# A branch prefetch hint, a new order of the up/gate steps, and the general path moved, in the experts of a 512-token layer pair

## The chip, the core and the metric

The kernel is one program on one core of a Trainium2 chip. The time is that of the device for one execution, in microseconds (us); lower is better. Engine names: PE is TensorE (PEld its weight loads), DVE is VectorE, ACT ScalarE, POOL GpSimd, SP SyncE, which here mainly starts DMAs. A "q" behind a name (PEq) is that engine's sequencer, which takes instructions in order, runs branches, and hands the rest to the engine.

## The reference, cut to what matters

All of it is fp32: a first layer (state-space mixer, gated convolution, MLP), a second one with a delta-rule mixer, and at its end a mixture of experts. Only the last is touched by the change:

```
N_GROUPS, EXPERTS_PER_GROUP, TOP_K = 4, 8, 2          # 32 experts, T = 512 tokens, D = 1024, D_EXPERT = 512
pg_top, g_top = lax.top_k(softmax(xf @ w_group + b_group), 1)
pe_top, e_top = lax.top_k(softmax(el_g), TOP_K)        # two experts of the token's group
wts = pg_top * pe_top / sum(pe_top)
hid = silu(xb @ w_gate[e]) * (xb @ w_up[e])            # xb: the tokens that chose expert e
out[token] += (hid @ w_down[e]) * wts
```

How many tokens an expert gets depends on the data, so the kernel must handle any count.

## The kernel before

**Stages.** The dense layers take the first 1,436 us of the profiled span. Then one Python loop (line 1964 on) lays out 32 experts, one after the other, i = 0 to 31; pair p = i // 2, place in the pair h = i % 2. Here "even" experts are the first of a pair (h = 0), "odd" ones the second.

**One expert.** SP loads six chunks of 1 MB (`load`: up and gate for k 0 to 3, up and gate for k 4 to 7, two of down) into a ring of 15 chunk buffers; a chunk's DMA waits until PE has used the buffer's last content. `gate_up` (L1722) multiplies the first 64 slots of the expert by up and gate (tile `gu`, 16 fp32 matmuls, two side by side in the array), ACT takes SiLU of the gate half (L1733), DVE multiplies (L1734) into `gh`. Then comes the branch `longer` (L1891): `tc.If(nx > 0)` at L1893, where `nx` is the number of 32-slot blocks that the expert has beyond its first 64 slots. If it has none, every engine jumps over the body; if it has one, an inner branch (L1894) takes `block_up`/`block_down`; if more, `wide_up`/`wide_down`. Behind the branch `hidden` transposes `gh` on PE (tile `tr`, L1741) and ACT copies it (`hT`), `outputs` multiplies by down (tile `dn`, L1753, 8 fp32 matmuls), DVE scales the result (L1757) and POOL scatters it to DRAM (`yd`).

**What else stands behind the branch on PE.** Even experts: `per_slot` (tile `cb`, L1666) turns the one-hot matrix `oh1`, which DVE builds (`places`, L1789 and L1792), into the token list of the next pair. Odd experts: `columns` (tile `xt`, L1716) transposes the next pair's 128 gathered rows, which ACT reads (L1719), `prepare` (L1807) transposes 64 more, and two `per_slot`.

**Order.** PE's instructions keep the order in which the program is written (`manual_schedule`); on the other engines a scheduler orders them inside a block between branches. Every engine has its own copy of each branch and jumps by itself.

**The last expert.** `longest` (L1946) handles counts beyond what `longer` holds, in a branch of its own (L1948) ahead of the last expert's `gate_up`. Its body holds a loop for each of the 32 experts. `read_back` (L1942) adds the scattered outputs, read back in four chunks (`yd`), to the residual; the last pair is not scattered but added by matmuls (`combined`).

Of the kernel before, what the change touches and what calls it, by code (L numbers as in the profile page):

```python
# [84 lines left out]
class Kern:  # L85
# [1377 lines left out]
    def route(self, lt_ps, r2):  # L1463
# [12 lines left out]
        self.extra = lp.tile([1, 33], I32, name="extra")  # L1476
# [132 lines left out]
    def moe(self, out):  # L1609
# [15 lines left out]
        def t_(tag, shape, dt=F32, bufs=1, pool=mp):  # L1625
            return pool.tile(shape, dt, tag=tag, bufs=bufs, name=self.nm(tag))
# [95 lines left out]
        def gate_up(ws, xs, s0, gh, tag="gu", bufs=1, between=(), start=4):  # L1722
# [12 lines left out]
            for fn in between:  # L1735
                fn()

        def hidden(gh, put=V.tensor_copy):
            pt = p_("tr", 1)
# [57 lines left out]
        def ranks(p):  # L1797
            return self.rank[:, :, expert(2 * p):expert(2 * p) + 9:8]

        gh, gh2 = r1[:, 2], t_("gh2", [P, 512])  # L1800
        xb1 = t_("xb1", [P, 8, 64])

        def prepare(r):

            ps = p_("xt", 2)
            for k in range(8):
                M.transpose(ps[:, 64 * k:64 * k + 64], xt1[r:r + 64, k * P:k * P + P], self.ident[r:r + 64, r:r + 64])  # L1807
            return ps

        def normed(ps, xb):  # L1810
            S_ = [P, 8, 64]
            V.tensor_tensor(xb, ps.rearrange("p (k s) -> p k s", k=8), self.gs[:, 0].unsqueeze(2).broadcast_to(S_), op=ALU.mult)
            V.tensor_tensor(xb, xb, self.gs[:, 1].unsqueeze(2).broadcast_to(S_), op=ALU.add)
            return xb
# [60 lines left out]
        def vals(p):  # L1875
            return self.vals[:, :, p]

        def wide_up(ws):
            gate_up(ws, normed(prepare(64), t_("xb2", [P, 8, 64])), 0, gh2, "cb", 3)

        def wide_down(ws, w):
            for fn in combined([down(ws, hidden(gh2), w[:, 1:2], w[:, 0:1], yx, "b")]):
# [6 lines left out]
        def longer(i, ws, nx, first, xb, far):  # L1889
            w, sx = first[0], first[2]  # L1890
            if sx is not None:  # L1891
                sx = sx[:, i % 2:i % 2 + 1]
            with tc.If(nx > 0):  # L1893
                with tc.If(nx > 1) as more_:  # L1894
                    hb = block_up(ws, xb, i % 2)
                    wide_up(ws)
                    block_down(ws, w[:, i % 2], hb, i % 2, sx)
                    wide_down(ws, far[1][:, i % 2])
                    with ExitStack() as ies:
                        for b in range(1, INLINE):  # L1900
                            ies.enter_context(tc.If(nx > 1 + 2 * b))
                            far = further(per_slot(places(ranks(i // 2), 96 + 64 * b, 64, "b"), vals(i // 2)))
                            rows2(far, i % 2)
                            wide_up(ws)
                            wide_down(ws, far[1][:, i % 2])
# [24 lines left out]
        oh1, oh2 = places(ranks(0), 64, 32, "b"), places(ranks(0), 96, 64, "2")  # L1930
        firsts, far = [], None

        def ahead():
# [2 lines left out]
            firsts.append(more(0, per_slot(oh1, vals(0))))  # L1936
            far = further(per_slot(oh2, vals(0)))

        def read_back(tl, t):

            for j in range(2):
                V.tensor_add(acc[:, t], acc[:, t], tl[:, j])  # L1942

        def longest():

            last = 1 + 2 * INLINE  # L1946
            c = self.chunk
            with tc.If(most > last):  # L1948
                for i in range(32):
                    nx = length(i)  # L1950
                    with tc.If(nx > last):
                        self.chunk = c
                        ws = load(i)
                        rc = t_("rc", [P, 4, 2])
                        V.tensor_scalar(rc, ranks(i // 2), -32.0 * last, None, op0=ALU.add)
                        with tc.For_i(last, nx, 2):
                            V.tensor_scalar(rc, rc, -64.0, None, op0=ALU.add)
                            far = further(per_slot(places(rc, 0, 64, "b"), vals(i // 2)), "3")
                            rows2(far, i % 2)
                            wide_up(ws)  # L1960
                            wide_down(ws, far[1][:, i % 2])

        pair, back = [], []
        nx = length(0, engines=engs)
        for i in range(32):
            p, h = divmod(i, 2)
            if h == 0 and p < 14:
                oh = onehot(p + 2)
            ws = load(i)
            if i == 31:  # L1970
                for t in range(4):
                    if t == 3:
                        longest()
                    back.append(chunk("yd").rearrange("p (c d) -> p c d", c=2))
                    nc.sync.dma_start(back[t], self.yd.rearrange("(c t p) d -> t p c d", c=2, p=P)[t])
                for t in range(2):
                    read_back(back[t], t)
            if i:
                with tc.If(length(i, engines=[mybir.EngineType.Pool]) > 1):
                    rows2(far, h)  # L1980
            if h and p < 15:
                oh2 = places(ranks(p + 1), 96, 64, "2")
            gate_up(ws, xs, 64 * h, gh, between=[] if i else [ahead], start=4 if i else 1)
            if i == 0:
                with tc.If(length(0, engines=[mybir.EngineType.Pool]) > 1):
                    rows2(far, 0)
                xb = normed(prepare(0), xb1)
            nx0, nx = nx, length(i + 1, engines=engs) if i < 31 else None
            longer(i, ws, nx0, firsts[p], xb, far)
            if h == 0 and p < 15:  # L1990
                oh1 = places(ranks(p + 1), 64, 32, "b")
            pw = pw1 = pw2 = ps = None
            if h and p < 15:
                columns()
                ps = prepare(0)
                if p < 14:
                    pw = per_slot(oh, vals(p + 2))
            hT = hidden(gh, A.copy)
            if p < 15:
                if h == 0:  # L2000
                    pw1 = per_slot(oh1, vals(p + 1))
                else:
                    pw2 = per_slot(oh2, vals(p + 1))
            w, sx = wv[p]
            if p < 15:
                scatter(sx[:, h:h + 1], outputs(ws, hT, w[:, h, 1:2]), 2)
            else:
                pair.append(down(ws, hT, w[:, h, 1:2], w[:, h, 0:1], yr[:, h]))
            if ps:
                xb = normed(ps, xb1)  # L2010
            if pw:
                wv.append(fetch(pw))
            elif i == 29:
                nc.scalar.dma_start(xt, ins["final_g_2"].rearrange("(a d) -> a d", a=1).to_broadcast([P, D]))
            if pw1:
                firsts.append(more(p + 1, pw1))
            if pw2:
                far = further(pw2)
            if i == 29:
                most = nc.values_load(self.extra[0:1, 32:33], min_val=0, max_val=14)  # L2020
            if i == 31:
                ob = t_("oh2", [P, T], F32R)
                V.tensor_scalar(ob, iota, firsts[p][1], None, op0=ALU.is_equal)
                pair.append((ob, yyb))
                for t in range(2, 4):
                    read_back(back[t], t)
        mes.close()

        fg, sq = xt, xs.rearrange("p k s -> p (k s)")
# [66 lines left out]
```

## Time and profile before

| | |
|---|---|
| time, median of 3 runs (range) | 2119.67 us (2109.05 to 2122.25) |
| profiled execution: its own time | 2119.71 us |
| profiled execution: span, first to last instruction | 2117.9 us |
| mean granted clock of PE | 0.90 of full |
| PE / PEld / DVE / ACT / POOL busy over the span | 86% / 56% / 53% / 28% / 15% |
| experts (1436 to 2083 us): PE busy | 524.5 of 647.0 us |
| experts: DMA share, granted clock | 0.81, 0.84 |

[...]

### The profile page before, as it was taken

To read this page: it belongs to the slowest core of one execution; us is meant where nothing else is said; L and a number is where in the kernel's file an instruction comes from. 1 tells how busy PE (TensorE), PEld (TensorE's weight loads), DVE (VectorE), ACT (ScalarE), POOL (GpSimd) and SP (SyncE) were. 2 spreads that over 40 slices of the span, in tenths; PEclk is the share of its full clock that TensorE was granted. 3 is DMA by queue.
4 is the path that set the end of the run, shared out by engine and by line. 5 is a ranking of instruction groups with operands and counts; after the bars stand their busy time and mean duration, and the time that the engine had idled before them with its cause. 6 is when DMAs were issued, how large, how long until landed. Compare 5 with 4: busy or idle time off the path is not lost. (4 is left out here: it accounts for less than half of the span.)

```text
span 2117.9 us, 24494 instructions
## 1 busy us (share of the span) xinstructions
PE 1821.1 (86%) x9177; PEld 1183.4 (56%) x9177; DVE 1126.3 (53%) x2238; ACT 586.2 (28%) x991; POOL 322.5 (15%) x209
## 2 busy tenths in 40 slices
PE   6868879799999999999899889977888788787884
PEld 4535556466777887777666668853333333333331
DVE  5799998634445654944676976643222222222225
ACT  3213223322433452323355332341111111111112
POOL 0343434410000000000122320210001111010000
PEclk9878889899999999999898989986888898888888
DMA  5111111248554332222221110357898788487874
GB/s 147 60 40 60 40 60 60 90 171 289 170 196 153 107 100 80 80 80 80 80 80 40 47 56 12 135 222 294 337 355 351 281 344 339 185 347 279 351 279 160
DMA packets 150214, 351.33 MB, mean 166 GB/s; under 512 B 20408, under 2 KB 107009, under 8 KB 130156
## 3 DMA queue, kind: packets, MB, share of 16 engines
q1 hardware_dynamic: 135533, 302.52, 39.3%
q0 software_dynamic: 8928, 33.37, 4.3%
q10 hardware_dynamic: 5534, 12.54, 1.6%
q8 instruction: 136, 2.23, 0.4%
q14 instruction: 83, 0.67, 0.1%
HBM read 339.63 MB, written 18.89 MB: 169 GB/s over the span
## 5 line engine op out<-in xcount | busy, mean ns | idle before, releaser
L125 ACT CAST wh<-w 128x1024 fp32r<-128x1024 f32 (+1 forms) x184 | 179.3, 975 | 415.3 <-PE acc L131 347.6
L126 POOL TENSOR_TENSOR wl<-w,wh 128x1024 fp32r<-128x1024 f32 (+1 forms) x76 | 183.6, 2421 | 620.7 <-PE acc L138 368.5
L1731 PE MATMUL gu<-ew,moe 128*64 128x512 f32 x1024 | 230.8, 604 | 3.1 <-PEq L1948 2.8
L126 DVE TENSOR_TENSOR wl<-w,wh 128x1024 fp32r<-128x1024 f32 (+1 forms) x108 | 123.3, 1141 | 119.1 <-PE acc L138 88.6
L1753 PE MATMUL dn<-ew,hT 128*64 128x512 f32 x528 | 173.0, 816 | 0.8 <-DVE hT L1744 0.4
L1731 PEld LDWEIGHTS gu<-ew,moe 128*64 128x64 f32 x1024 | 73.8, 139 | 153.4 <-issue 152.0
L130 PE MATMUL acc<-xH,wh 128*128 128x512 f32 x352 | 150.5, 428 | 0.0
L131 PE MATMUL acc<-xL,wh 128*128 128x512 f32 x352 | 147.1, 418 | 0.0
L1733 ACT ACTIVATE moe<-gu 64x512 f32<-64x512 f32 x32 | 18.9, 592 | 406.5 <-PE gu L1731 384.1
L1734 DVE TENSOR_TENSOR moe<-gu,moe 64x512 f32<-64x512 f32 x32 | 21.8, 682 | 197.7 <-ACTq L1893 123.6
L130 PE MATMUL acc<-fH,wh 128*128 128x512 f32 x256 | 103.7, 406 | 0.4 <-ACT fH L152 0.4
L138 PE MATMUL acc<-xH,wl 128*128 128x512 f32 x352 | 97.1, 421 | 7.6 <-DVE wl L126 4.8
L130 PE MATMUL acc<-gH,wh 128*128 128x512 f32 x256 | 103.2, 403 | 0.0
L1753 PEld LDWEIGHTS dn<-ew,hT 128*64 128x64 f32 x528 | 47.6, 187 | 99.4 <-issue 97.4
L131 PE MATMUL acc<-fL,wh 128*128 128x512 f32 x256 | 102.2, 399 | 0.0
L131 PE MATMUL acc<-gL,wh 128*128 128x512 f32 x256 | 102.0, 398 | 0.0
L130 PEld LDWEIGHTS acc<-xH,wh 128*128 128x128 f32 x352 | 71.1, 202 | 41.8 <-issue 19.6
L138 PEld LDWEIGHTS acc<-xH,wl 128*128 128x128 f32 x352 | 71.1, 203 | 25.8 <-DVE wl L126 5.3
L131 PEld LDWEIGHTS acc<-xL,wh 128*128 128x128 f32 x352 | 71.0, 202 | 21.7 <-issue 6.6
L1757 DVE SCALAR_TENSOR_TENSOR moe<-dn,wv,moe 128x512 f32<-128x512 f32 x33 | 24.8, 751 | 108.9 <-PE dn L1753 67.7
L130 PE MATMUL acc<-hxH,wh 128*128 128x512 f32 x160 | 71.6, 452 | 2.1 <-DVE y L1248 2.1
L1700 POOL DMA_INDIRECT yd<-moe,sx x30 | 29.9, 998 | 274.7 <-DVE moe L1757 218.7
(710 smaller groups left out, 3522.7 us busy)
## 6 DMA issues: line engine op xcount, KB each, us to landing
ew<-in_w_up_dram SPq DMA_DIRECT2D x64, 1024.0 KB
ew<-in_w_gate_dram SPq DMA_DIRECT2D x64, 1024.0 KB
ew<-in_w_down_dram SPq DMA_DIRECT2D x64, 1024.0 KB
w<-in_w_in_dram SPq DMA_DIRECT2D x36, 1024.0 KB
w<-in_w_ff_dram SPq DMA_DIRECT2D x32, 1024.0 KB
wm<-in_w_mod_dram POOLq DMA_DIRECT2D x24, 1024.0 KB, 6.2
xt<-in_x_dram SPq DMA_DIRECT2D x8, 512.0 KB
w<-in_w_conv_out_dram SPq DMA_DIRECT2D x4, 1024.0 KB
```

The source lines that it names most:

```text
L125: nc.scalar.copy(H[:, :kt], W[:, :kt, c:c + P])
L126: self.lsub.tensor_sub(L[:, :kt], W[:, :kt, c:c + P], f(H[:, :kt]))
L130: self.nc.tensor.matmul(ps, H[:, k], aH[:, k, sl], start=(k == 0), stop=False)
L131: self.nc.tensor.matmul(ps, H[:, k], aL[:, k, sl], start=False, stop=False)
L138: nc.tensor.matmul(ps, L[:, k], aH[:, k, sl], start=False, stop=(k == kt - 1))
L1700: nc.gpsimd.indirect_dma_start(out=self.yd.rearrange("r (m c) -> (r m) c", m=m), out_offset=bass.IndirectOffsetOnAxis(ap=sx, axis=0), in_= ...
L1731: M.matmul(gu[64 * j:64 * j + 64], xs[:, k, s0:s0 + 64], ws[2 * (k // 4) + j][:, k % 4], start=(k == 0), stop=(k == 7), tile_position=(0, ...
L1733: A.activation(gh[64:], gu[64:], AF.Silu)
L1734: V.tensor_mul(gh[:64], gu[:64], gh[64:])
L1753: M.matmul(dn[64 * j:64 * j + 64], hT[:, q], ws[4 + q // 2][:, q % 2, 512 * j:512 * j + 512], start=(q == 0), stop=(q == 3), tile_position ...
L1757: V.scalar_tensor_tensor(y, dn, wsl, m5, op0=ALU.mult, op1=ALU.mult)
```

## The change

`gate_up` takes the eight k steps in the order 0, 4, 1, 5, 2, 6, 3, 7 instead of 0 to 7. Behind its first step it emits one instruction on PE, a branch prefetch hint, that names the expert's branch (`label`). `longest` loses its own branch ahead of the last `gate_up`: the last expert's `longer` and `longest` stand together under one `tc.If(some > 0)`, where `some` (computed in `route`) is above zero if the last expert has extra blocks or some expert has more than `longer` holds. `fetch_back(3)`, the fourth read of `yd`, follows that branch. For even experts DVE's `places` for `oh1` stands ahead of the branch, into a buffer of its own tag, and `per_slot` of it ahead of `hidden`. The wide path takes `gh` from the tag of `xb2`; `gh2` is gone.

```diff
         V.tensor_copy(self.extra[:, 32:33], q)
+
+        V.tensor_scalar(q, q, -1.0 - 2 * INLINE, 0.0, op0=ALU.add, op1=ALU.max)
+        V.tensor_add(self.extra[:, 33:34], q, ov[:, 31:32])
...
-            for k in range(8):
-                if k >= start:
-                    for fn in between[:3 if k < 6 else 1 if k == 6 else 0]:
+            for n, k in enumerate((0, 4, 1, 5, 2, 6, 3, 7)):
+                if n >= start:
+                    for fn in between[:3 if n < 6 else 1 if n == 6 else 0]:
...
-                    M.matmul(gu[64 * j:64 * j + 64], xs[:, k, s0:s0 + 64], ws[2 * (k // 4) + j][:, k % 4],
-                             start=(k == 0), stop=(k == 7), tile_position=(0, 64 * j), skip_group_check=True)
+                    mm = M.matmul(gu[64 * j:64 * j + 64], xs[:, k, s0:s0 + 64], ws[2 * (k // 4) + j][:, k % 4],
+                                  start=(n == 0), stop=(n == 7), tile_position=(0, 64 * j), skip_group_check=True)
+                if n == 0 and label:
+                    with tc.issue_after(mm.ins):
+                        tc.mark_branch_hint_location(label, engines=[mybir.EngineType.PE])
...
-            with tc.If(nx > 0):
+            with tc.If(nx > 0, label=label):
...
             if i == 31:
-                for t in range(4):
-                    if t == 3:
-                        longest()
-                    back.append(chunk("yd").rearrange("p (c d) -> p c d", c=2))
-                    nc.sync.dma_start(back[t], self.yd.rearrange("(c t p) d -> t p c d", c=2, p=P)[t])
-                for t in range(2):
-                    read_back(back[t], t)
+                for t in range(3):
+                    fetch_back(t)
+                with tc.high_priority():
+                    for t in range(2):
+                        read_back(t)
+            if h == 0 and 0 < p < 15:
+                oh1 = places(ranks(p + 1), 64, 32, "1")
...
-            gate_up(ws, xs, 64 * h, gh, between=[] if i else [ahead], start=4 if i else 1)
+            gate_up(ws, xs, 64 * h, gh, between=[] if i else [ahead], start=4 if i else 1, label=f"long{i}")
...
-            longer(i, ws, nx0, firsts[p], xb, far)
-            if h == 0 and p < 15:
-                oh1 = places(ranks(p + 1), 64, 32, "b")
+            if i < 31:
+                longer(i, ws, nx0, firsts[p], xb, far, f"long{i}")
+            else:
+                with tc.If(some > 0, label="long31"):
+                    longer(i, ws, nx0, firsts[p], xb, far)
+                    with tc.If(most > 1 + 2 * INLINE):
+                        longest()
+                fetch_back(3)
...
+            if h == 0 and p < 15:
+                pw1 = per_slot(oh1, vals(p + 1))
             hT = hidden(gh, A.copy)
-            if p < 15:
-                if h == 0:
-                    pw1 = per_slot(oh1, vals(p + 1))
-                else:
-                    pw2 = per_slot(oh2, vals(p + 1))
+            if h and p < 15:
+                pw2 = per_slot(oh2, vals(p + 1))
```

On PE, from the join behind expert 2's branch to the start of expert 3's `gate_up`, the kernel before has these rows (`ew_...` are the weight chunks):

```order
L1893 UNCONDITIONAL_BRANCH
L1979 UNCONDITIONAL_BRANCH
L1741 MATMUL tr_11363<-pk,moe_9939 128x64 x4
L1666 MATMUL cb_11371<-vals,ohb_11358 128x6 x4
L1753 MATMUL dn_11376<-ew_11000,hT_11368 64x512
L1861 UNCONDITIONAL_BRANCH
L1753 MATMUL dn_11376<-ew_11000,hT_11368 64x512 x3
L1753 MATMUL dn_11376<-ew_11002,hT_11368 64x512 x4
L1731 MATMUL gu_11448<-ew_11418,moe_9942 64x512
L1731 MATMUL gu_11448<-ew_11420,moe_9942 64x512
L1731 MATMUL gu_11448<-ew_11418,moe_9942 64x512
L1731 MATMUL gu_11448<-ew_11420,moe_9942 64x512
```

and the changed kernel, at the same place:

```order
L1904 UNCONDITIONAL_BRANCH
L1991 UNCONDITIONAL_BRANCH
L1669 MATMUL cb_11373<-vals,oh_1619_11011 128x6 x4
L1872 UNCONDITIONAL_BRANCH
L1752 MATMUL tr_11378<-pk,moe_9941 128x64 x4
L1764 MATMUL dn_11386<-ew_11007,hT_11383 64x512 x4
L1764 MATMUL dn_11386<-ew_11009,hT_11383 64x512 x4
L1735 MATMUL gu_11458<-ew_11428,moe_9944 64x512
L1735 MATMUL gu_11458<-ew_11430,moe_9944 64x512
L2110 BRANCH_PREFETCH_HINT
L1735 MATMUL gu_11458<-ew_11432,moe_9944 64x512
L1735 MATMUL gu_11458<-ew_11434,moe_9944 64x512
```

The `cb` matmuls now stand ahead of the `tr` transposes; in the next `gate_up` the hint stands behind the first step, and the second step already reads the second two chunks.

On DVE, at the last expert, the kernel before has:

```order
L1948 UNCONDITIONAL_BRANCH x2
L1979 UNCONDITIONAL_BRANCH
L1734 TENSOR_TENSOR moe_9939<-gu_28209,moe_9939 64x512
L1942 TENSOR_TENSOR x_9490<-x_9490,yd_23702 128x1024 x2
L1942 TENSOR_TENSOR x_9490<-x_9490,yd_23704 128x1024 x2
L1887 TENSOR_LOAD extra
L1893 COMPARE_AND_BRANCH
L1894 COMPARE_AND_BRANCH
```

and the changed kernel:

```order
L1768 SCALAR_TENSOR_TENSOR moe_9941<-dn_23782,wv_22486,moe_9941 128x512
L1779 TENSOR_TENSOR moey<-moe_9941,moey 64x512 x2
L1744 TENSOR_TENSOR moe_9941<-gu_23834,moe_9941 64x512
L1956 TENSOR_TENSOR x_9490<-x_9490,yd_23810 128x1024 x2
L1956 TENSOR_TENSOR x_9490<-x_9490,yd_23812 128x1024 x2
L2037 TENSOR_LOAD extra
L2038 TENSOR_LOAD extra
L1898 TENSOR_LOAD extra
L2005 COMPARE_AND_BRANCH
```

The product (L1734, now L1744) still stands ahead of the four additions of `read_back`; two register loads are added, and the branch behind them now spans the general path, which stood ahead of the product before.

## Rows read from the trace of the kernel before

**Rows 1.** Windows view, experts: us; busy us (instructions) by engine; PEclk, DMA share, GB/s
```profile
1436.00:2083.00 647.00, 524.50 (x2540) 223.24 (x2538) 161.63 (x558) 83.60 (x234) 58.62 (x54) 0.84 0.81 314
```

**Rows 2.** Waits of PE, 1400 to 2118: who waited for whom, us in total, times, longest
```profile
PE xt L1716 <- PEq L1893: 39.7, 15, 3.3
PE tr L1741 <- PEq L1893: 13.7, 5, 3.5
...
PE tr L1741 <- DVEq L1893: 11.6, 4, 6.5
...
PE tr L1741 <- DVE moe L1734: 6.5, 2, 3.3
...
PE tr L1741 <- issue: 5.2, 1, 5.2
PE cb L1666 <- issue: 4.3, 2, 2.9
...
PE gu L1731 <- PEq L1948: 2.8, 1, 2.8
...
PE tr L1741 <- DVE rkb L1789: 2.1, 1, 2.1
```

**Rows 3.** Instructions of line 1893: count, ns min/median/max, first and last start
```profile
L1893 PEldq COMPARE_BRANCH  x32: 82/5716/6739, 1447.5 to 2078.7; - x32
...
L1893 PEldq EVENT_SEMAPHORE  x28: 51/51/51, 1453.3 to 2083.2; - x28
```

**Rows 4.** Timeline of PE, experts 3 and 4: start, us, what, xcount, [idle before]
```profile
1508.36 1.07 PE L1716 MATMUL xt<-pk,moe 128*128 128x128 f32 x8 [2.67 <-PEq L1893]
...
1513.79 5.69 PE L1753 MATMUL dn<-ew,hT 128*64 128x512 f32 x16
1519.31 7.03 PE L1731 MATMUL gu<-ew,moe 128*64 128x512 f32 x32
1529.58 0.43 PE L1741 MATMUL tr<-pk,moe 64*128 64x64 f32 x4 [3.23 <-DVE moe L1734]
...
1530.54 5.35 PE L1753 MATMUL dn<-ew,hT 128*64 128x512 f32 x16
1535.72 7.04 PE L1731 MATMUL gu<-ew,moe 128*64 128x512 f32 x32
```

**Rows 5.** Timeline, all engines, expert 30 and the start of expert 31
```profile
2058.60 7.03 PE L1731 MATMUL gu<-ew,moe 128*64 128x512 f32 x32
...
2067.26 0.43 PE L1741 MATMUL tr<-pk,moe 64*128 64x64 f32 x4 [1.62 <-DVEq L1893]
...
2068.08 3.65 PE L1753 MATMUL dn<-ew,hT 128*64 128x512 f32 x16 [0.40 <-ACT hT L1744]
...
2074.52 8.65 PE L1731 MATMUL gu<-ew,moe 128*64 128x512 f32 x32 [2.78 <-PEq L1948]
```

**Rows 6.** Page, part 5: busy us, mean ns | idle before, what ended it
```profile
L1753 PE MATMUL dn<-ew,hT 128*64 128x512 f32 x528 | 173.0, 816 | 0.8 <-DVE hT L1744 0.4
```

**Rows 7.** Timeline of PE, experts 1 and 21, from `xt` to `dn`
```profile
1470.84 1.94 PE L1716 MATMUL xt<-pk,moe 128*128 128x128 f32 x8 [2.78 <-PEq L1893]
...
1477.07 3.56 PE L1753 MATMUL dn<-ew,hT 128*64 128x512 f32 x8
...
1889.60 1.07 PE L1716 MATMUL xt<-pk,moe 128*128 128x128 f32 x8 [1.89 <-PEq L1893]
...
1894.34 6.56 PE L1753 MATMUL dn<-ew,hT 128*64 128x512 f32 x16
```

**Rows 8.** Instructions of line 1948 on DVE, as in rows 3
```profile
L1948 DVEq EVENT_SEMAPHORE  x2: 21/21/21, 2079.2 to 2079.3; - x2
...
L1948 DVEq COMPARE_BRANCH  x1: 56/56/56, 2074.3 to 2074.3; - x1
```

**Rows 9.** Timeline, all engines, behind expert 31's up/gate
```profile
2084.61 4.88 DVE L1942 TENSOR_TENSOR x<-x,yd 128x1024 f32<-128x1024 f32 x4
2089.70 0.66 PE L1741 MATMUL tr<-pk,moe 64*128 64x64 f32 x4 [6.53 <-DVEq L1893]
```

More of the change, by code (lines that the diff above doesn't have):

```diff
@@ L1475, in route @@
         self.toks = lp.tile([P, 4, 2], F32R, name="toks")
-        self.extra = lp.tile([1, 33], I32, name="extra")
+        self.extra = lp.tile([1, 34], I32, name="extra")
         self.both = lp.tile([1, 16], I32, name="both")
@@ L1720, in columns, with gate_up @@
                                  bias=self.gs[:, 1, kk:kk + 1])
-        def gate_up(ws, xs, s0, gh, tag="gu", bufs=1, between=(), start=4):
+        def gate_up(ws, xs, s0, gh, tag="gu", bufs=1, between=(), start=4, label=None):
             gu = p_(tag, bufs)
             between = list(between)
-            for k in range(8):
-                if k >= start:
-                    for fn in between[:3 if k < 6 else 1 if k == 6 else 0]:
+            for n, k in enumerate((0, 4, 1, 5, 2, 6, 3, 7)):
+                if n >= start:
+                    for fn in between[:3 if n < 6 else 1 if n == 6 else 0]:
                         fn()
@@ L1736, in gate_up @@
                 fn()
+            return gh
         def hidden(gh, put=V.tensor_copy):
@@ L1878, in wide_up, with wide_down @@
         def wide_up(ws):
-            gate_up(ws, normed(prepare(64), t_("xb2", [P, 8, 64])), 0, gh2, "cb", 3)
-        def wide_down(ws, w):
-            for fn in combined([down(ws, hidden(gh2), w[:, 1:2], w[:, 0:1], yx, "b")]):
+            return gate_up(ws, normed(prepare(64), t_("xb2", [P, 512]).rearrange("p (k s) -> p k s", k=8)), 0, None, "cb", 3)
+        def wide_down(ws, w, gh):
+            for fn in combined([down(ws, hidden(gh), w[:, 1:2], w[:, 0:1], yx, "b")]):
                 fn()
@@ L1887, in length, with longer @@
             return nc.values_load(self.extra[0:1, e:e + 1], min_val=0, max_val=14, **kw)
-        def longer(i, ws, nx, first, xb, far):
+        def longer(i, ws, nx, first, xb, far, label=None):
             w, sx = first[0], first[2]
@@ L1892, in longer @@
                 sx = sx[:, i % 2:i % 2 + 1]
-            with tc.If(nx > 0):
+            with tc.If(nx > 0, label=label):
                 with tc.If(nx > 1) as more_:
                     hb = block_up(ws, xb, i % 2)
-                    wide_up(ws)
+                    g = wide_up(ws)
                     block_down(ws, w[:, i % 2], hb, i % 2, sx)
-                    wide_down(ws, far[1][:, i % 2])
+                    wide_down(ws, far[1][:, i % 2], g)
                     with ExitStack() as ies:
@@ L1903, in longer @@
                             rows2(far, i % 2)
-                            wide_up(ws)
-                            wide_down(ws, far[1][:, i % 2])
+                            wide_down(ws, far[1][:, i % 2], wide_up(ws))
                 with more_.Else():
@@ L1929, in moe @@
         columns()
-        oh1, oh2 = places(ranks(0), 64, 32, "b"), places(ranks(0), 96, 64, "2")
+        oh1, oh2 = places(ranks(0), 64, 32, "1"), places(ranks(0), 96, 64, "2")
         firsts, far = [], None
@@ L1937, in ahead, with fetch_back, read_back @@
             far = further(per_slot(oh2, vals(0)))
-        def read_back(tl, t):
+        def fetch_back(t):
+            back.append(chunk("yd").rearrange("p (c d) -> p c d", c=2))
+            nc.sync.dma_start(back[t], self.yd.rearrange("(c t p) d -> t p c d", c=2, p=P)[t])
+        def read_back(t):
             for j in range(2):
-                V.tensor_add(acc[:, t], acc[:, t], tl[:, j])
+                V.tensor_add(acc[:, t], acc[:, t], back[t][:, j])
         def longest():
@@ L1947, in longest @@
             c = self.chunk
[L1948 to L1961, printed above, removed]
+            for i in range(32):
+                nx = length(i)
+                with tc.If(nx > last):
+                    self.chunk = c
+                    ws = load(i)
+                    rc = t_("rc", [P, 4, 2])
+                    V.tensor_scalar(rc, ranks(i // 2), -32.0 * last, None, op0=ALU.add)
+                    with tc.For_i(last, nx, 2):
+                        V.tensor_scalar(rc, rc, -64.0, None, op0=ALU.add)
+                        far = further(per_slot(places(rc, 0, 64, "b"), vals(i // 2)), "3")
+                        rows2(far, i % 2)
+                        wide_down(ws, far[1][:, i % 2], wide_up(ws))
         pair, back = [], []
@@ L2020, in moe @@
                 most = nc.values_load(self.extra[0:1, 32:33], min_val=0, max_val=14)
+                some = nc.values_load(self.extra[0:1, 33:34], min_val=0, max_val=28)
             if i == 31:
@@ L2025, in moe @@
                 for t in range(2, 4):
-                    read_back(back[t], t)
+                    read_back(t)
         mes.close()
```

5 lines of the change are left out of this document (4 added, 1 removed).

## The prediction

> **What bounds the kernel now.** Start with the share of each resource in the experts, the only part that the change touches [rows 1]: TensorE is busy 524.5 of 647.0 us, so it idles 122.5 us, at a mean granted clock of 0.84; the DMA engines are at 0.81. Neither is full. The next view is who ended TensorE's idle time [rows 2]. The first name is not a weight transfer but TensorE's own sequencer at L1893, the join behind each expert's branch: 39.7 us in 15 waits ahead of `xt` (odd experts), and in even experts several names ahead of `tr`, which are the same place. No row of that view holds a wait for `ew` worth a term, so the weights arrive in time.
>
> The instructions of L1893 show what the place is [rows 3]: 32 compare-branches on PE's sequencer with a median of 5716 ns, the shortest 82 ns. The join's semaphore instruction stands 28 times: 28 experts jump over the body, 4 enter it. The jump is the dear one: the sequencer runs it while up/gate matmuls are still queued, so that of 5.7 us only about 2.65 us (39.7 / 15) show as idle time. I read it as code that is not at hand at the jump's target and has to be fetched.
>
> The timeline of one pair shows what the idle time costs beyond itself [rows 4]. Expert 3: up/gate ends at 1505.69 (2.67 ahead of `xt` at 1508.36), and `dn` starts at 1513.79, a pause of 8.1 us without dense matmuls. Expert 4: 1526.34 to 1530.54, a pause of 4.2. Behind both, `dn` takes 5.69 and 5.35 us. Expert 30 is the natural experiment [rows 5]: up/gate ends at 2065.63, `tr` follows after 1.62, `dn` after 2.45 in all, and `dn` takes 3.65 us. [...] So a short pause left the clock up, and the longer ones were followed by the lower level. In expert 30, `tr` names DVE: it waits for `gh`, that is ACT's SiLU and DVE's product. 1.62 us is what is left of an even expert's gap when the branch costs nothing that shows.
>
> **The change part by part.** *The hint.* It is issued at the start of up/gate, the branch near its end; up/gate is 7.03 us long [rows 4], a cold branch 5.7 [rows 3], so the fetch fits ahead of the jump if it starts with the first step. I take it that it works, and then what is left is expert 30's gap in even experts and almost nothing in odd ones, since `xt` needs no result of up/gate.
> - Odd, 15 waits: 39.7 us now; I leave 0.25 each (bounds 0 and 0.5, a few sequencer instructions of 51 ns as in [rows 3]): 39.7 - 3.7 = 36.0 saved.
> - Even, 12 waits ahead of `tr` [rows 2]: 13.7 + 11.6 + 6.5 + 5.2 + 2.1 = 39.1, less the last expert's 6.53, which is another thing [rows 9]: 32.6. Left are 12 x 1.62 = 19.4: 13.2 saved.
> - Two waits of `cb` named "issue", 4.3 us: a second stall shortly behind a join, which I put down to the block that follows the target. The sequencer will now stand at the join, waiting for up/gate to end, while that block comes: 4.3 saved (0 if not).
> - L1948, the branch ahead of the last `gate_up`, goes: 2.8 saved [rows 2].
>
> *`per_slot` ahead of `hidden`.* In even experts `cb` now runs in the 1.62 us in which PE waits for `gh`; its input `oh1` is made by DVE during up/gate, where DVE is mostly idle (161.6 us busy of 647 [rows 1]). Before, `tr` to `dn` took 0.96 (1529.58 to 1530.54 [rows 4]); without `cb` between, 0.82 (2067.26 to 2068.08 [rows 5]): 0.14 x 11 = 1.5 saved.
>
> *The order 0, 4, 1, 5.* It needs all four chunks from the second step on, where before the last two were needed halfway, 3.5 us later. Cost 0 as long as the weights are early, which the absence of such waits in [rows 2] says. If DMA became the bound, up to 3.5 us of an expert's cover would be gone.
>
> *The last expert.* DVE's jump over the general path stood ahead of the last product: branch at 2074.3, next instruction at 2079.2, 4.9 us [rows 8], at a time when DVE had nothing to do. It now stands behind product and additions, and `tr` waits for DVE's join there: already now it starts at 2089.70, right behind the additions' end at 2089.49 [rows 9]. So the 4.9 us land on the path. At best the fetch starts with the last of the four additions (4.88 / 4 = 1.2 us earlier): bounds 3.7 and 4.9, and two more register loads on DVE without a price here. I take 4.5 lost. `high_priority` does not help: the additions still stand behind the product. The hint is for PE only.
>
> Sum of the gaps: 36.0 + 13.2 + 4.3 + 2.8 + 1.5 = 57.8 saved, 4.5 lost.
>
> *The clock.* All `dn` records together take 173.0 us for 33 experts' worth (528 records of 16) [rows 6]; at 3.65 each they would take 120.4, so 52.6 us are due to the lower level. The small work of odd experts, `xt` to `dn`, takes 6.2 us in expert 1 (1470.84 to 1477.07) and 4.7 in expert 21 (1889.60 to 1894.34), where the gap ahead was 1.89 and the clock still up [rows 7]: up to 1.5 x 15 = 22. The last up/gate takes 8.65 instead of 7.03 behind the 2.78 us gap [rows 5]: 1.6. Bounds: 0 and 76. What comes back? Even experts will pause about 2.45 us, like expert 30, most of them without a drop; odd ones still about 5 us (0.25 + 4.7), longer than the 4.2 that cost expert 4 its clock. So I take 15 of the 52.6 (mostly even experts), 10 of the 22, and the 1.6: 26.6.
>
> Total: 57.8 + 26.6 - 4.5 = 80 saved. From the profiled execution's own 2119.71 (2117.9 of span and 1.8 around it; the median is 2119.67, so it is a typical run): 2040.
>
> *The next bound.* DMA was busy 0.81 of 647.0 = 524 us, and the same bytes remain, so the experts can't get shorter by more than 123 us. 80 leaves 43 us of idle DMA in the stage; transfers will wait more for each other, but PE should not wait for weights.
>
> [...] The rows show a jump to cold code at 5.7 us [rows 3]. [...]
>
> **The rivals.**
> - *The clock does not follow.* The gaps shrink, but odd and even pauses of 2.4 to 5 us still drop it: 57.8 - 4.5 = 53 saved, 2066. For it: 5 us is over expert 4's 4.2. Against: expert 30.
> - *The clock follows everywhere, DMA ends it.* 57.8 + 76 - 4.5 = 129, over the DMA bound of 123 less the tail's 4.5: about 2001, and some `gu` would wait for `ew`.
> - *The hint does nothing.* The jump stays cold. L1948's gap and the slow last up/gate (2.8 + 1.6) pay for the tail (4.5), `cb` in the gap brings 1.5: 2118. [...]
> - *Slower: the hinted block pushes out one that PE needs in sequence.* Place: inside up/gate or at the join. Price: one more stall like those of L1893, 2.65 us [rows 2], for each expert where a block boundary falls there, with the jump still cold. Against the nil of the third rival it decides from 8 experts on (21 us, 1%); with 14 of 28 it is 37 us: 2155. Against it: up/gate shows no stall of its own (7.03 and 7.04 us [rows 4]), so sequential blocks come well ahead.
>
> **How the numbers follow.** Forecast (2020 to 2056) 0.46; the clock does not follow 0.20; DMA bound 0.13; no effect 0.13; slower 0.08. A measurement of this kernel can tell about 1% (21 us) from no change. Faster by over 1%: 0.46 + 0.20 + 0.13 = 0.79; within 1%: 0.13; slower: 0.08. The range holds the first three, from 2000 (DMA bound) to 2095 (the clock does not follow and only half of the gaps close: 53 / 2 = 27 saved, 2093): 0.8. The likeliest case is 2040.
>
> **What would show it.** L1893's compare-branches on PE: a median far under 5.7 us if the hint works, unchanged if not. The waits of `xt` for L1893: about 4 us in total instead of 39.7. `tr` in even experts 1.6 us behind up/gate, named DVE. `dn` in total: near 158 us as forecast, 173 if the clock does not follow, 125 if it follows everywhere. `tr` of the last expert about 11 us behind up/gate instead of 6.5. Granted clock above 0.84 in the experts, DMA share above 0.9. It is wrong if L1893 stays above 5 us, if a wait for `ew` of more than a few us in total appears, or if up/gate itself gets longer than 7.03.

## The result, and the profile after

The changed kernel takes 2049.72 us (median of 4 runs, 2048.06 to 2055.29), the kernel before 2116.70 (4 runs, 2109.05 to 2122.25): a ratio of 0.9707, 95% interval 0.9682 to 0.9732, so 2.9% or 67 us faster. The forecast was 2040 with a range of 2000 to 2095. The profiled execution took 2055.29 us (span 2053.5) against 2119.71 (span 2117.9), and the traces below have these 64.4 us to explain, where the forecast's sum was 80.

The hint does what it says. The instructions of line 1904 (the old 1893; count, ns min/median/max, first and last start) answer to [rows 3]:

```profile
L1904 PEldq COMPARE_BRANCH  x31: 74/449/3735, 1439.8 to 1997.2; - x31
```

The median fell from 5716 to 449 ns. The waits of PE from 1380 us on (who waited for whom: us in total, times, longest) answer to [rows 2]:

```profile
PE xt L1719 <- DVEq L1904: 21.8, 13, 1.8
PE xt L1818 <- ACT moe L1722: 17.4, 15, 1.2
PE cb L1669 <- DVEq L1904: 16.8, 9, 2.3
PE tr L1752 <- DVEq L2005: 9.4, 1, 9.4
...
PE cb L1669 <- ACTq L1904: 1.7, 2, 0.9
...
PE xt L1719 <- PEq L1904: 0.3, 1, 0.3
```

PE's own sequencer (PEq) has nearly gone from this view: 39.7 us became 0.3. In its place stands DVE's sequencer at the same branch, 21.8 us ahead of `xt` and 16.8 ahead of `cb`. The old wait had covered a new one. The windows view of the experts answers to [rows 1], the page's row of `dn` (part 5) to [rows 6]:

```profile
1436.00:2017.00 581.00, 492.37 (x2524) 200.22 (x2520) 158.76 (x550) 81.01 (x224) 57.84 (x54) 0.89 0.89 349
```

```profile
L1764 PE MATMUL dn<-ew,hT 128*64 128x512 f32 x528 | 170.3, 805 | 6.7 <-ACT hT L1755 5.9
```

The stage is 66 us shorter, PE's mean granted clock in it, as a share of full speed, rose from 0.84 to 0.89 and the DMA share, the mean busy share of the core's 16 DMA engines, from 0.81 to 0.89. But `dn` still takes 170.3 us, hardly less than the 173.0 of before.

**What the new wait is.** PE's timeline has two odd experts of the changed kernel that differ: expert 3, whose up/gate ends at 1489.09, and expert 7, whose ends at 1551.81.

```profile
1489.40 1.07 PE L1719 MATMUL xt<-pk,moe 128*128 128x128 f32 x8 [0.31 <-PEq L1904]
...
1553.39 1.06 PE L1719 MATMUL xt<-pk,moe 128*128 128x128 f32 x8 [1.57 <-DVEq L1904]
```

DVE's join behind the branch in the same two experts, and between them ACT's join in expert 3, from the instructions of line 1904:

```profile
L1904 DVEq EVENT_SEMAPHORE  x1: 21/21/21, 1483.1 to 1483.1; - x1
...
L1904 ACTq EVENT_SEMAPHORE  x1: 17/17/17, 1489.8 to 1489.8; - x1
...
L1904 DVEq EVENT_SEMAPHORE  x1: 21/21/21, 1553.3 to 1553.3; - x1
```

In expert 3, DVE passed its join at 1483.1, long before up/gate's end, and `xt` starts 0.31 us behind that end. In expert 7, DVE's product stands ahead of its branch; the join comes at 1553.3, and `xt` starts right behind that. ACT's join is not what `xt` waits for: in expert 3 it comes at 1489.8, after `xt` has started at 1489.40. (`cb` does wait for ACT's join too, in two experts: the 1.7 us of the view.) The scheduler moves the product across the branch: it is behind it in experts 1 to 4, ahead from expert 5 on, which makes 13 odd experts, the 13 waits of the view.

All of the 64.4 us, summed from PE's timeline by kind of expert (us; "gap" runs from up/gate's end to the next work on PE, "small work" from there to `dn`):

| | before | changed |
|---|---|---|
| 15 odd experts: gap / small work / `dn` | 39.7 / 87.7 / 82.9 | 22.4 / 70.8 / 81.8 |
| 11 even experts: gap / small work / `dn` | 29.2 / 17.6 / 54.4 | 17.8 / 17.7 / 54.8 |
| even experts as a whole, with the next up/gate | 181.3 | 165.9 |
| 4 experts with extra blocks, as a whole | 120.5 | 113.2 |
| expert 0's up/gate; from its end to expert 1's | 13.7; 18.6 | 9.2; 16.7 |
| from the last up/gate's end to the kernel's end | 34.7 | 37.8 |

Odd experts gave 35.2 us, even 15.4, those with extra blocks 7.3, expert 0 6.4; the end took 3.1. The remaining 3.2 us are in the dense layers, which the change doesn't touch.

### The profile page after: what moved, and what is told of

It is laid out like the page before. It is cut to its first block, busy times and chain, and to the rows that moved or that the text cites. A ratio compares the mean times of both kernels' runs of the same rounds, so it can differ in the third digit from the quotient of the medians.

```text
span 2053.5 us, 24514 instructions
## 1 busy us (share of the span) xinstructions
PE 1795.8 (87%) x9177; PEld 1163.0 (57%) x9177; DVE 1118.4 (54%) x2240; ACT 586.2 (29%) x991; POOL 321.4 (16%) x209
## 3 DMA queue, kind: packets, MB, share of 16 engines
q8 instruction: 126, 2.06, 0.4%
## 5 line engine op out<-in xcount | busy, mean ns | idle before, releaser
L1735 PE MATMUL gu<-ew,moe 128*64 128x512 f32 x1024 | 225.9, 593 | 0.4 <-ACT moe L1722 0.4
L1764 PE MATMUL dn<-ew,hT 128*64 128x512 f32 x528 | 170.3, 805 | 6.7 <-ACT hT L1755 5.9
L1744 DVE TENSOR_TENSOR moe<-gu,moe 64x512 f32<-64x512 f32 x32 | 21.8, 683 | 193.9 <-ACTq L1904 121.1
L131 PEld LDWEIGHTS acc<-xL,wh 128*128 128x128 f32 x352 | 73.0, 207 | 22.4 <-issue 6.6
```

What stands on the lines that cost most here:

```text
L131: self.nc.tensor.matmul(ps, H[:, k], aL[:, k, sl], start=False, stop=False)
L1735: mm = M.matmul(gu[64 * j:64 * j + 64], xs[:, k, s0:s0 + 64], ws[2 * (k // 4) + j][:, k % 4], start=(n == 0), stop=(n == 7), tile_position ...
L1764: M.matmul(dn[64 * j:64 * j + 64], hT[:, q], ws[4 + q // 2][:, q % 2, 512 * j:512 * j + 512], start=(q == 0), stop=(q == 3), tile_position ...
```

## The experiments

After the result the theory had two parts: the hint alone brought the gain, and what was left of the gaps is DVE's join behind DVE's product. Its rivals: the other edits have a share in the gain; the new wait is for something else that ends at the same time. The ratios are to the kernel before.

**e1: without the hint.**

```
-                if n == 0 and label:
-                    with tc.issue_after(mm.ins):
-                        tc.mark_branch_hint_location(label, engines=[mybir.EngineType.PE])
```

> The changed kernel with only the prefetch hint taken out. Theory (the hint brings the whole gain): the branch on PE's sequencer has a median above 5 us again, and the time is 2113 to 2125, since what is left of the change gives back as much (the branch ahead of the last up/gate, 2.8 us, and the slow up/gate behind it, 1.6) as it takes (the last expert's tr waits 9.4 us instead of 6.5). Rival (the new order of steps and per_slot in the pause bring a good part of the 67 us): 2070 to 2095, with gaps ahead of xt and cb that are shorter than before although the branch is as long.

Measured 2112.45 us, ratio 0.9991 (0.9963 to 1.0019): the whole gain is gone. Its branch and its waits of PE:

```profile
L1900 PEldq COMPARE_BRANCH  x31: 82/6024/6750, 1436.5 to 2051.9; - x31
...
PE xt L1719 <- PEq L1900: 41.2, 15, 3.3
PE cb L1669 <- PEq L1900: 23.3, 9, 4.2
```

The gaps are back under their old name, and what is left of the change moves nothing that can be measured.

**e2: only the hint, in the kernel before** (the label on the branch and the hint behind up/gate's first step).

> The kernel before with only the hint added (the steps in the order 0 to 7, the general path in its own branch, per_slot behind the transposes). Theory (hint alone): the branch at about 0.45 us, and 2045 to 2058: the gain of the hint less the branch ahead of the last up/gate, plus the 3 us that the last expert loses in the changed kernel. Rival (the hint needs the other edits, for instance the block of code laid out otherwise): above 2080.

Measured 2056.99 us, ratio 0.9707 (0.9649 to 0.9764), the changed kernel's ratio to the last digit. With e1 this settles it: the hint is the gain. The waits of PE carry two more readings:

```profile
PE tr L1744 <- DVEq L1896: 24.9, 11, 6.5
PE xt L1716 <- DVEq L1896: 22.3, 13, 1.8
...
PE gu L1731 <- PEq L1951: 3.1, 1, 3.1
```

DVE's join appears here too, 13 times ahead of `xt`. And the general path in its own branch costs 3.1 us ahead of the last up/gate but leaves `tr` of the last expert at 6.5 instead of 9.4: about an exchange at par.

**e3: the steps in the order 0 to 7** (`enumerate(range(8))` in `gate_up`).

> The changed kernel with up/gate's steps in the order 0 to 7. Theory: within 5 us of the changed kernel, 2045 to 2055, since no matmul of up/gate waits for a weight chunk in either. Rival (the order sets when chunks come free and so the DMA's pace): more than 10 us slower or faster, and waits of up/gate for ew in the trace.

Measured 2051.95 us, ratio 0.9694 (0.9644 to 0.9743): the order makes no difference, as forecast.

**e4: SiLU and product behind the branch** (the edit, shortened).

```
-            A.activation(gh[64:], gu[64:], AF.Silu)
-            V.tensor_mul(gh[:64], gu[:64], gh[64:])
+            def finish():          # traced behind `longer`, experts 0 to 30
+                a = A.activation(gh[64:], gu[64:], AF.Silu)
+                v = V.tensor_mul(gh[:64], gu[:64], gh[64:])
+                for x, y in zip((a, v), self.behind):      # last instruction of the body on ACT, DVE
+                    tc.add_manual_dep(x.ins, y.ins.name, NoSync ...)
```

> The changed kernel with SiLU on ACT and the product on DVE issued behind the expert's branch instead of ahead of it (experts 0 to 30), so that both engines run through their branch while up/gate still computes. Theory (PE's xt and cb wait for DVE's join, which stands behind the product: 21.8 us in 13 waits and 16.8 in 9): the wait of odd experts falls from 1.6 to about 0.3 us and cb slips into the 1.6 us in which tr waits for gh: 2018 to 2030. The four experts that enter the body pay up to 1.5 us each for a later gh. Rival (xt and cb wait for something else that ends at the same time, a PSUM buffer read by the product, say): the waits stay and are named product, 2045 to 2055. Rival (a shorter pause also keeps the clock up): dn in total well under 170 us, 2000 to 2015.

Measured 2025.00 us, ratio 0.9574 (0.9512 to 0.9636), inside the theory's range. The waits of PE:

```profile
PE tr L1761 <- DVE moe L1746: 26.6, 16, 3.2
...
PE cb L1669 <- PEq L1914: 5.9, 10, 3.1
...
PE xt L1719 <- PEq L1914: 4.7, 15, 0.4
```

`xt` waits 4.7 us in all instead of 22.1, by PE's own join: only the order on ACT and DVE was changed, and the wait of `xt` went instead of taking the product's name. That shows the first half of e4's theory. The second half, on even experts, fell: `cb` starts early, but `tr` now waits for the product. The timeline of expert 6, whose up/gate ends at 1535.10, shows why:

```profile
1535.15 0.59 ACT L1745 ACTIVATE moe<-gu 64x512 f32<-64x512 f32 x1 [10.52 <-PE gu L1735]
...
1535.41 0.58 PE L1669 MATMUL cb<-vals,oh 128*128 128x6 f32 x4 [0.31 <-PEq L1914]
...
1536.03 0.16 DVE L1679 TENSOR_SCALAR idx<-cb 128x1 int32<-128x1 f32 x1 [6.97 <-PE cb L1669]
...
1536.31 0.41 DVE L1812 TENSOR_TENSOR oh<-pk,rk 128x256 fp32r<-128x256 f32 x1
1536.75 0.68 DVE L1746 TENSOR_TENSOR moe<-gu,moe 64x512 f32<-64x512 f32 x1
...
1537.58 0.43 PE L1761 MATMUL tr<-pk,moe 64*128 64x64 f32 x4 [1.59 <-DVE moe L1746]
...
1538.41 5.35 PE L1773 MATMUL dn<-ew,hT 128*64 128x512 f32 x16 [0.40 <-ACT hT L1764]
```

SiLU ends at 1535.74, but DVE's queue now holds work on the new `cb` ahead of the product, which starts at 1536.75, one us late. `dn` starts 3.31 us behind up/gate, no sooner than the 3.18 of the changed kernel. The wait had changed its owner. The four experts with extra blocks took 121.5 us instead of 113.2, some 2 each where up to 1.5 was expected. `dn` took 158.0 us in all instead of 170.3, and the experts' mean granted clock was 0.91 instead of 0.89, so some of the clock came back, but the time of the second rival, 2000 to 2015, was not met.

**e5 and e9: the hint later** (`if n == 7 and label`, `if n == 4 and label`), **e6: the hint one expert early** (each expert's hint names the next expert's branch).

> The changed kernel with the hint behind the last step of up/gate instead of behind the first, so that it is issued less than 1 us ahead of the branch instead of about 8. Theory (a hint starts a fetch that takes about 5 us until the jump is free): the branch takes 5 us less the lead, a median of 4 to 5 us; since it is issued 3.7 us ahead of up/gate's end and DVE's join is 1.6 us behind that end, hardly anything of it shows: 2045 to 2062. Rival (a hint so late is none: the branch stays at 5.7 or more and a second fetch of the same code may stand in its way): 2085 or above.

> The changed kernel with each hint naming the branch of the next expert instead of its own, so some 17 us ahead instead of 8 (expert 0 has none). Theory (a hinted block is kept only until the code that runs in sequence asks for its own blocks; between this hint and its branch lies an expert's worth of code and another jump): the branches are cold again, median above 5 us, and the time is 2105 to 2125, slower than without hint if the vain fetches stand in the way. Rival (the block is kept until its jump): branches at 0.45 us, 2045 to 2058.

> The changed kernel with the hint behind the fifth of the eight steps instead of the first. What the runs so far show: a lead of 6.5 us and more between hint and branch gives a branch of 0.45 us nearly always; a lead of 0.8 us left 6.1 us, as without hint. Theory (the fetch that a hint starts counts only when it is done; a jump that comes earlier starts over): with a lead of 3 to 4 us the branches stay near 6 us, and 2100 to 2118. Rival (a jump joins a fetch that is under way): branches of 1.5 to 3 us, hidden by the queue ahead of up/gate's end, 2045 to 2060.

The compare-branches on PE, first of e5, then of e6, then of e9:

```profile
L1904 PEldq COMPARE_BRANCH  x31: 74/6078/7083, 1439.4 to 2055.5; - x31
```

```profile
L1904 PEldq COMPARE_BRANCH  x31: 73/522/6783, 1442.5 to 2021.8; - x31
```

```profile
L1904 PEldq COMPARE_BRANCH  x31: 74/2967/6064, 1436.0 to 1998.4; - x31
```

- e5: 2112.63 us, ratio 0.9984 (0.9958 to 1.0009). The hint is issued 0.79 us ahead of the branch and brings nothing; the theory's 2045 to 2062 was wrong, the rival right. The theory had let the hint's fetch pay for the lead, and reckoned the rest away behind the queue.
- e9: 2065.07 us, ratio 0.9774 (0.9741 to 0.9806). The lead is 3.27 us, the branch 2.97: together 6.2, about what a cold jump takes (6.02 in e1). A jump that joins a fetch under way would take just that: the theory is wrong, the rival's branch of 1.5 to 3 us right, its time 5 us too low. In its trace the two waits for DVE's join are those of the changed kernel (21.8 us in 13, 16.8 in 9), and the profiled execution took 2056.22; the other runs took up to 13 us more, and why, this trace can't show.
- e6: 2073.41 us, ratio 0.9810 (0.9770 to 0.9849), between the two theories. Of 27 taken branches, 13 are cheap (under 0.6 us) and 14 take over 5. Expert 0 has no hint here, so a hinted block lives through an expert's worth of code and another jump in 13 of 26 cases. The dear ones are all experts with i mod 4 = 3 or 0, the cheap ones, but for expert 12, those with 1 or 2: where the branch lies in the code seems to decide, but why is not explained.

The DMA records show the mechanism. The blocks that belong to PE's jumps are of 16,384 bytes, on a queue that carries nothing else (`q8 instruction`, 136 packets with 2.23 MB before, 126 with 2.06 MB in the changed kernel; start in us, then line or bytes, and duration). In the kernel before, a jump's block begins to arrive 3.7 us into the jump; in the changed kernel, the block comes 3.8 us behind the hint, and the jump 5.5 us later finds it there:

```
before   1560.63 COMPARE_BRANCH L1893 6.05
         1564.36 DMA q8 16384 1.02
changed  1575.17 BRANCH_PREFETCH_HINT L2110 0.04
         1578.93 DMA q8 16384 1.03
         1584.40 COMPARE_BRANCH L1904 0.36
```

All jumps of the two kernels agree with these: one that has to wait ends 2.3 to 2.9 us behind the start of a block, hinted or not (28 jumps before, 9 changed). In e5 the block begins to arrive some 3.6 us into the jump, as in e1 without a hint.

**e7: as e4, expert 31 too. e8: as e7, with one hint on DVE for the last branch.**

> As e4, and the same for expert 31: SiLU and product behind its branch too, so that on DVE the four additions and the jump over the general path run during the last up/gate, with the product last. Theory (tr of the last expert waits 9.5 us for additions, jump and join on DVE in turn): the additions end about 2 us before up/gate does, the jump's 3.2 us then end about 3 us behind it, and the product follows: tr 4 to 5.5 us behind up/gate instead of 9.5, 4 to 5 us less than e4, 2018 to 2022. Rival (the additions wait for yd from memory, not for the product): tr stays at 9 us or more, 2025.

> As e7, and one more prefetch hint, on DVE, for the last branch, issued ahead of the four additions. Theory (DVE's jump over the general path is cold code as PE's jumps were): DVE's jump falls from 3.2 us to under 0.5, tr of the last expert 1.6 to 2.5 us behind up/gate's end, 2.5 to 3 us less than e7, 2015 to 2020. Rival (the additions end too late or the hint does nothing on DVE): as e7.

2026.39 us, ratio 0.9596 (0.9564 to 0.9627), and 2026.80, ratio 0.9592 (0.9560 to 0.9623): neither differs from e4, and both theories missed. The end of e7, where up/gate ended at 1999.49:

```profile
1995.55 4.88 DVE L1966 TENSOR_TENSOR x<-x,yd 128x1024 f32<-128x1024 f32 x4
...
2005.70 1.62 PE L1799 MATMUL cb<-moey,oh 128*128 128x512 f32 x3 [6.21 <-DVEq L2016]
2005.76 0.68 DVE L1746 TENSOR_TENSOR moe<-gu,moe 64x512 f32<-64x512 f32 x1 [5.33 <-DVEq L2016]
...
2007.25 0.69 PE L1761 MATMUL tr<-pk,moe 64*128 64x64 f32 x4
```

The additions did move into up/gate's time, but DVE stood idle for 5.33 us at its jump (3.21 in the changed kernel) and three `cb` matmuls went ahead of `tr`: 7.76 us behind up/gate instead of 9.4. The DVE hint of e8 took DVE's idle time ahead of the product from 5.33 to 4.55 us only, with 6.3 us of lead. A block (8,192 bytes, as on the second instruction queue, q14, with 81 packets and 0.66 MB in the changed kernel) came 3.3 us behind that hint, but another one 2.6 us into the jump, and the jump ended 1.8 us later. Why the hint does so much less there than on PE stays open.

**e10: as e7, with the four additions on POOL** (`nc.gpsimd.tensor_tensor(..., op=ALU.add)` in `read_back` for t < 2).

> As e7 (SiLU and product behind the branch in every expert, the last too), with the four additions of the first two read-back chunks on POOL instead of DVE, so that DVE has nothing ahead of its last branch but the work of expert 30. Theory (in e7 tr of the last expert came 7.7 us behind up/gate because additions, jump and join followed each other on DVE): DVE's jump is over before up/gate ends, tr comes 1.5 to 3 us behind it; 4 to 6 us less than e7, about 2021. Rival (the fourth read-back chunk, whose load now waits for POOL's jump, or the additions on DVE that share memory with POOL's, end later by as much): 2024 to 2030.

2022.31 us, ratio 0.9576 (0.9545 to 0.9606). The trace does what the theory says: `tr` comes 1.65 us behind up/gate (which ended at 1983.74), and the end takes 31.8 us instead of 37.8.

```profile
1984.56 0.68 DVE L1746 TENSOR_TENSOR moe<-gu,moe 64x512 f32<-64x512 f32 x1 [2.76 <-ACT moe L1745]
...
1985.39 0.43 PE L1761 MATMUL tr<-pk,moe 64*128 64x64 f32 x4 [0.26 <-DVE moe L1746]
```

The intervals of e4, e7 and e10 overlap, so the time alone shows no gain. One part of the rival is in the trace too: while POOL adds, DVE is slower. The same two operations of DVE in e7, then in e10, where POOL's first addition starts 0.46 us into them:

```profile
1994.11 1.40 DVE L1788 TENSOR_TENSOR moey<-moe,moey 64x512 fp32r<-64x512 f32 x2 [0.68 <-ACT moey L1787]
```

```profile
1978.36 3.45 DVE L1788 TENSOR_TENSOR moey<-moe,moey 64x512 fp32r<-64x512 f32 x2 [0.68 <-ACT moey L1787]
```

**e12: as e10, with DVE's work on `cb` and the one-hot matrices held behind the product** (the same kind of order-only dependency, on five operations in `index`, `listed`, `more` and `places`).

> As e10, and DVE's work that needs even experts' cb (the next token list, the next one-hot matrices) is held behind DVE's product. In e4 and e10 those five or six operations slipped ahead of the product, since cb now runs at once, and the product came 1.0 us later than SiLU would have let it: dn started 3.3 us behind up/gate's end in even experts, where expert 30, which has no such work, needed 2.3 to 2.45. Theory: dn of even experts starts 2.4 to 2.5 us behind up/gate's end, 0.85 us less in 11 experts, 9 us: 2010 to 2016. Rival (the pause only changes its owner, since tr waits for something else, or the clock takes it back): dn at 3 us or more, 2018 to 2026.

2000.19 us, ratio 0.9456 (0.9431 to 0.9480): 22 us less than e10 where 6 to 12 were expected. Expert 6, whose up/gate ends at 1536.35:

```profile
1536.66 0.58 PE L1669 MATMUL cb<-vals,oh 128*128 128x6 f32 x4 [0.31 <-PEq L1922]
...
1537.03 0.68 DVE L1753 TENSOR_TENSOR moe<-gu,moe 64x512 f32<-64x512 f32 x1 [6.74 <-ACT moe L1752]
1537.64 0.14 DVE L1686 TENSOR_SCALAR idx<-cb 128x1 int32<-128x1 f32 x1
...
1537.86 0.43 PE L1769 MATMUL tr<-pk,moe 64*128 64x64 f32 x4 [0.61 <-DVE wv L1693]
```

`dn` starts 2.33 us behind up/gate in all 11 even experts (3.46 on average in e10): 12.5 us, of which 2.5 are expert 4's, whose hinted jump took 6.04 us in e10. The clock added to it (the experts' mean granted clock is 0.94 instead of 0.92): `dn` of even experts takes 45.2 us in all instead of 53.3, with 8 of 11 at the full 3.65 us instead of 5. That is the part that the expectation left out. It is not shown that the shorter pause brought it: in e7, where most of these pauses were 3.31 us, 8 of 11 ran at 3.65 too. And the two profiled executions differ by 14.9 us (2017.35 and 2002.42), so the traces don't hold all of the 22.

**e13: as e12, with the inner branch's two cases exchanged in the code** (`tc.If(nx > 1, preferred_fallthrough_block=False)`).

> As e12, with the inner branch laid out so that the case of one extra block follows on without a jump, and the jump stands behind that block instead (three experts: 10, 14 and 22, whose inner jump has no hint and takes 5.6 to 6.1 us, 2.5 of it ahead of the body's first matmul). Theory: the body starts right behind up/gate, 2.5 us less in three experts, and the jump behind it hides behind the body's last matmuls and the 1.6 us in which tr waits for the product: 4 to 7 us less than e12. Rival (the jump is as cold at its new place, and the code that now lies ahead moves blocks so that others grow cold): as e12 or slower.

1992.60 us (1989.72 to 1995.14), ratio 0.9430 (0.9410 to 0.9450). The waits of PE in e12 have the gap ahead of the extra blocks:

```profile
PE dn L1850 <- issue: 7.6, 3, 2.7
```

In e13 it is gone in all three experts, as the theory says. The intervals of e12 and e13 overlap, so the 7.6 us between their medians are likely but not shown by the time alone. e13 is 5.7% faster than the kernel before and beats the changed kernel. Its windows view of the experts, from 1431 us on (expert 0 starts at 1423):

```profile
1431.00:1954.00 523.00, 465.56 (x2518) 187.25 (x2514) 156.14 (x533) 79.89 (x222) 60.30 (x55) 0.93 0.96 385
```

The DMA share is at 0.96, so little is left there before the transfer of the weights bounds the stage, although no `gu` waits for `ew` yet.

## Why the forecast held, and where it was 10 us off

The direction, the cause and the range were right: the jump's code is fetched ahead, and the median branch fell below 0.5 us. How close the sum came is in part luck, as the end of this section shows. The rival in which the hint does nothing is out: e1 and e2 differ from their partners by the hint alone, and 60 us hang on it. The other rivals: that the clock does not follow was nearly so for `dn` (170.3 us, where 173 stood for it) and not for the small work; up/gate takes 105.5 us in odd experts in both kernels, so nothing shows a needed block pushed out, and no wait for `ew` came up, so DMA did not end it.

The steps of the sum, against the two profiled executions:

| step | forecast | measured |
|---|---|---|
| odd experts, gap ahead of `xt` | 36.0 saved | 17.3 saved (39.7 to 22.4) |
| even experts, up/gate's end to `dn` (the gap, `cb`'s second stall, `cb` in the gap: 13.2 + 4.3 + 1.5) | 19.0 saved | 11.3 saved (46.8 to 35.5) |
| branch ahead of the last up/gate, and that up/gate itself | 4.4 saved | 4.5 saved |
| the end, without `dn` | 4.5 lost | 2.6 lost |
| clock in odd experts' small work | 10 saved | 16.9 saved |
| clock in `dn` | 15 saved | 2.7 saved (173.0 to 170.3) |
| expert 0 and the four with extra blocks, without `dn` | not in the sum | about 11 saved |
| dense layers, which the change leaves alone | not in the sum | 3.2 less |

- **The step that failed most** is "almost nothing in odd ones, since `xt` needs no result of up/gate". It needs no result, but it waits for DVE's join, and DVE gets there only when its product, which does need up/gate, is done. The bounds of 0 and 0.5 us were too narrow, since they came from PE's sequencer alone; 1.6 to 1.8 us stood there in 13 of 15 experts. e4 shows it: with the product behind the join the wait is 0.31 us, and the 15 waits sum to 4.7 us, where the forecast's residue was 3.7. Why PE waits for DVE's join at all can be argued from the code (the body's wide path lets DVE read buffers of the same tag as `xt` and `cb`), but no run tested it.
- **Even experts**: the forecast let `cb` run in the 1.62 us in which PE waits for `gh`. It did not: in 8 of the 11 `cb` waited for the same join, started 1.8 us behind up/gate and stood ahead of `tr`. Only with e4 and e12 together did the step come true, with `dn` at 2.33 us where the forecast's own model, expert 30, had 2.45.
- **The end**: the jump over the general path did land on the path, as written. It took 3.2 us instead of the 3.7 to 4.9 of the bounds.
- **The clock** came back where the forecast had less of it (small work of odd experts) and hardly in `dn`. The trace of the kernel before shows two levels of it under `dn`, as shares of full speed: in expert 3 the windows view has 0.50 in each of the first four us and 1.00 from 1518.8 on (0.64 over all 5.69 us), in expert 4 0.68 over 5.35 us, in expert 30 1.00 over 3.65 us. The forecast's first premise, pauses of 2.45 us in even experts, was not met: `dn` started 3.23 us behind up/gate on average, and 4 of 11 ran at 3.65. Its second, that expert 30 shows what a pause of 2.45 us does, fell too. In the changed kernel expert 30's up/gate ends at 2001.00, the pause is again 2.45 us, and `dn` takes 5.35 at a granted clock of 0.68:

```profile
2002.62 0.43 PE L1752 MATMUL tr<-pk,moe 64*128 64x64 f32 x4 [1.62 <-DVEq L1904]
...
2003.45 5.35 PE L1764 MATMUL dn<-ew,hT 128*64 128x512 f32 x16 [0.40 <-ACT hT L1755]
```

Odd experts 1 and 3 of that kernel paused for 4.6 us, and `dn` took 3.65 at 1.00. So the pause just ahead does not set the level by itself. Over whole kernels less pause did go with more clock (`dn` in all 170.3 us in the changed kernel, 154.6 to 158.0 in e4, e7, e8 and e10, 147.2 and 149.4 in e12 and e13), but what decides in a single expert stays open. That expert 0's first up/gate got 4.5 us faster was not foreseen; it differs between kernels that share all code ahead of it and differ by the hint's place alone (9.2 us in the changed kernel at a granted clock of 0.94, 13.5 in e9 at 0.63), so it is the clock and not an edit.

The errors partly cancelled: 26.4 us too much in the gaps and 12.3 in `dn`, against 6.9 too little in the small work, 11 not foreseen, 1.9 at the end and 3.2 in the dense layers: 15.7, about the difference of 80 and 64.4. Without what cancelled, the sum would have been some 39 us too high.

## What to carry to other kernels

When a wait is to be removed, ask for each instruction behind it what else it waits for, and when that comes at the earliest: the view of waits names only the last (here PE's 39.7 us ahead of `xt`, behind which DVE's 21.8 stood). At the join behind a branch one engine can wait for another to pass its own (`xt` for DVE's, up to 1.8 us in 13 experts), so let an engine run through its branch before the work that depends on the critical result, not after it (e4: 24.7 us less than the changed kernel). And give a branch hint early, a full cold jump ahead (6 us in these runs) where there is room: with 8.2 us of lead it was worth 60 us, with 3.3 most of that, with 0.8 nothing; one branch too early it worked in half of the cases.

## What the runs showed of the hardware

- An unhinted jump on PE took 5.0 to 6.7 us in 26 of 28 cases of the kernel before (3.3 and 3.8 in experts 30 and 31), a hinted one 0.45 at the median. At a lead of 3.27 us lead and jump add up to 6.2 us (3.27 + 2.97), as if they shared one fetch (a jump of e1, without hint, takes 6.02). At 0.79 they don't: 0.79 + 6.08 is 6.9, and the jump was no shorter than without a hint.
- A hint doesn't always help in time: 9 of the 27 taken branches of the changed kernel still took 1.0 to 3.7 us with leads of 6.5 to 9.3, hidden behind up/gate and DVE's join. All nine are experts with i mod 4 = 3 or 0. Their blocks began to arrive 5.1 to 10.5 us behind the hint, and the jump ended 2.4 to 2.5 us after that. In experts 20, 24 and 28 another block came 1.4 to 1.7 us behind the hint; in the other six none did, and what held theirs up stays open. In e4 a single jump (expert 16) took 6.51 us and showed as a gap of 3.1: a block had come 4.2 us behind its hint, but another came 4.0 us into the jump.
- DVE's jump over the general path kept it idle for 3.2 us (changed kernel), 5.3 (e7) and, with a hint 6.3 us ahead, 4.6 (e8). Over the bodies of the experts' branches, DVE and ACT got from branch to join in 0.2 to 0.6 us, so it is not the engine alone.
- DVE was slower while POOL added: in e10 two operations took 3.45 us instead of 1.40, and two of its own additions 2.1 and 3.3 us instead of 1.2.
